# The order of wide and narrow matmuls in three of the seven quarter products of a feed-forward pair

## The chip, the cores and the metric

The kernel runs on one core of a Trainium2 chip. Its metric is the device time of one execution in microseconds; the profile comes from one further execution of the same program. TensorE is called PE below, VectorE DVE, ScalarE ACT, GpSimd POOL and SyncE SP, as the profile does.

## What is computed

One block of a streaming encoder on 512 frames of 1024 features, in float32: a feed-forward half step, a mixer (convolution module and gated linear attention), a second feed-forward half step, a gated embedding and a last norm. The change touches the feed-forward blocks alone, of which there are two:

```python
def _swiglu(x, w_in, w_out):
    gate, up = jnp.split(x @ w_in, 2, axis=-1)
    return (jax.nn.silu(gate) * up) @ w_out
...
h = h + 0.5 * _swiglu(_rmsnorm(h, ffn1_norm[i]), ffn1_w_in[i], ffn1_w_out[i])
...
h = h + 0.5 * _swiglu(_rmsnorm(h, ffn2_norm[i]), ffn2_w_in[i], ffn2_w_out[i])
```

`x` is 512 x 1024, `w_in` 1024 x 5632 (gate and up side by side) and `w_out` 2816 x 1024.

## The kernel before

**Two parts for each operand.** A float32 value is held as a high part (rounded by an ACT copy) and a low part (what is left, by a DVE subtraction). A product is high by high, high by low and low by high. For weights the tiles are `wh` and `wl`, each in a ring of six buffers.

**Pairs.** The hidden width 2816 is worked through in 11 pairs of 128-column blocks, each with its gate and its up columns. For a pair the 2 x 2 block product (gate and up rows by the two halves of the frames) is formed by a scheme with seven quarter products in place of eight: `m1`, `m2`, `m6`, `m7`, `m5`, `m4`, `m3`, in this order. Each multiplies a 512 x 256 piece of weights (raw, or a sum of pieces: `s1` to `s4`) with a 512 x 256 piece of activations (raw, `hg` in the rows of the profile, or a sum, `t1` to `t4`, shown as `t`). Results are kept in PSUM tiles of two banks (`pd`): `m1`, `m6`, `m5` and `m3` add into `p.x`, `m7` and `m4` into `p.w`, and `m2` stands in `p.y`.

**Late pairs.** From the third pair of the scheme on, a pair is "wide" (`p.wide`), and a quarter product is 16 matmuls written by `mul2`: eight *wide* ones, in which one high weight block `wh` (128 x 128) meets the high and low part of the activations side by side (512 columns), then eight *narrow* ones, in which the low block `wl` meets the high part alone (256 columns, into the first half of the same bank). Each matmul loads a weight block of its own. The first block has seven late pairs (4 to 10) and the second eight (3 to 10), 15 in all. Earlier pairs go through `mul`, where everything is 256 columns wide, unless the tile has two banks.

**What stands around.** After `m5` and after `m3` a late pair has an output piece: 24 matmuls with `w_out`, 512 columns each, into tiles `ps` (`second`). In rows of the profile these are `ps<-act,wh` and the like. After `m1`, `m6` and `m5` ACT copies `p.x` out of PSUM (`snap`), and after `m3` it copies a half of it; DVE adds these to `p.y` and `p.w` (`plus`).

**What sets the order.** `drive` runs the units (a quarter product or an output piece) in a list; it calls a unit's preparation, the high and low part of its weights, four units ahead (`AHEAD`; five for `m5`). Every PE, DVE and ACT instruction is chained behind the one recorded before it, so each engine keeps the order in which the code is written. Weights come by DMA issued from SP.

Of the kernel before, what the change touches and what calls it, by code (L numbers as in the profile page):

```python
# [31 lines left out]
HALF = SEQ // 2  # L32
# [30 lines left out]
def block_kernel(ctx: ExitStack, tc: tile.TileContext, a: dict, out: bass.AP):  # L63
    nc = tc.nc
    pe, dve, act, pool = (Ordered(tc, e) for e in (nc.tensor, nc.vector, nc.scalar, nc.gpsimd))
# [39 lines left out]
    def tmp(s, w=SEQ, dt=F32, bufs=2):  # L105
        return tp.tile([P, w], dt, tag=s, bufs=bufs, name=nm(s))
# [20 lines left out]
    def bank():  # L127
        if mode[0] == 0:
            turn_no[0] += 1
            at = turn_no[0] % 7  # L130
            if at in (3, 4):
                return fixed()
            if at in (5, 6):
                return spare()
        return psum(singles(), 3, [P, SEQ])
# [37 lines left out]
    first_of, at = {}, 0  # L173
# [49 lines left out]
    def high(r3):  # L223

        nk, nc_ = r3.shape[1], r3.shape[2]
        hi = wp.tile([P, 1024], F32R, tag="wh", bufs=6, name=nm("wh"))
        lo = wp.tile([P, 1024], F32R, tag="wl", bufs=6, name=nm("wl"))
        h3 = hi[:, :nk * nc_].rearrange("p (k c) -> p k c", k=nk)
        l3 = lo[:, :nk * nc_].rearrange("p (k c) -> p k c", k=nk)
        act.copy(h3, r3)  # L230
        return h3, l3, r3
# [116 lines left out]
    def mul(ps, w, x, first, last, ks=range(4)):  # L348

        (wh, wl), k0 = w, ks[0]  # L350
        for k in ks:
            xh, xl = x[k][:2]
            for i in range(2):
                cs = slice(i * P, (i + 1) * P)
                o = ps[:, i * HALF:(i + 1) * HALF]
                end = last and k == ks[-1] and i == 1
                pe.matmul(o, wh[:, k - k0, cs], xh, start=(first and k == ks[0] and i == 0), stop=False, skip_group_check=True)
                pe.matmul(o, wh[:, k - k0, cs], xl, start=False, stop=False, skip_group_check=True)
                pe.matmul(o, wl[:, k - k0, cs], xh, start=False, stop=end, skip_group_check=True)

    def two(t):
        return t.rearrange("p (k c) -> p k c", k=2)

    def mul2(ps, w, x, first, last):

        if len(ps.shape) == 2:
            return mul(ps, w, x, first, last)
        wh, wl = w
        at = [(k, i, slice(i * P, (i + 1) * P)) for k in range(4) for i in range(2)]
        for k, i, cs in at:  # L370
            pe.matmul(two(ps[:, i]), wh[:, k, cs], x[k][2], start=(first and k == 0), stop=False, skip_group_check=True)
        for k, i, cs in at:
            pe.matmul(ps[:, i, 0:HALF], wl[:, k, cs], x[k][0], start=False, stop=last and k == 3, skip_group_check=True)

    def sub(out, x, y):
        dve.tensor_tensor(out=out, in0=x, in1=y, op=ALU.subtract)
# [233 lines left out]
    def ffn(w_in, w_out, x, gname, given, first, rsb, hooks, plain, far={}, casts={}, adds=()):  # L610
# [6 lines left out]
        start = 1 + len(plain)  # L617
# [6 lines left out]
        def row(i):  # L624
            return got['rsb'][:, i * HALF:(i + 1) * HALF].unsqueeze(1).to_broadcast([P, 2, HALF])

        def times_row(src, i, name):
            o = tmp(name)
            dve.tensor_tensor(out=two(o), in0=two(src), in1=row(i), op=ALU.mult)
            return o  # L630

        def silu(g):
            s = tmp("s")
            act.activation(s, g, AF.Silu)
            return s

        def plus(ps, t, i, name):
            o = tmp(name)
            if len(ps.shape) == 2:
                dve.tensor_tensor(out=o, in0=ps, in1=t, op=ALU.add)  # L640
            elif len(t.shape) == 2:
                dve.tensor_tensor(out=two(o), in0=ps[:, :, 0:HALF], in1=two(t), op=ALU.add)
                dve.tensor_tensor(out=two(o), in0=ps[:, :, HALF:], in1=two(o), op=ALU.add)
            else:
                dve.tensor_tensor(out=t, in0=ps, in1=t, op=ALU.add)
                dve.tensor_tensor(out=two(o), in0=t[:, :, 0:HALF], in1=t[:, :, HALF:], op=ALU.add)
            dve.tensor_tensor(out=two(o), in0=two(o), in1=row(i), op=ALU.mult)
            return o
# [11 lines left out]
        def snap(ps, name, rest=None):  # L660
            if name == "sq":
                o = rest if rest is not None else two(tmp(name, 2 * SEQ))
                if len(ps.shape) == 2 and rest is None:
                    act.copy(o[:, 0], ps)
                else:
                    act.copy(o, ps)
                return o
            o = tmp(name, bufs=1)
            act.copy(o, ps)
            return o  # L670

        def gated(p, s, u, i):
            if not hasattr(p, "m"):
                p.m = tmp("m", 2 * SEQ, bufs=1).rearrange("p (f c) -> p f c", f=2)
            dve.tensor_tensor(out=p.m[:, :, i * HALF:(i + 1) * HALF], in0=two(u), in1=two(s), op=ALU.mult)

        def act_parts(p):
            c = [c for c, (f0, f1) in enumerate(CUTS) if f0 <= p.f < f1][0]
            to = cvt if c % 2 == 0 and p.f == CUTS[c][0] else bt
            p.acts = [split(p.m[:, f, :], "act", to) for f in range(2)]  # L680
# [31 lines left out]
            return [gate0]  # L712

        def m6(p):
            mul2(p.x, p.part("s2"), x.op["t2"], False, False)
            p.u2 = snap(p.x, "sq" if p.wide else "u2")

        def m7(p):
# [1 line left out]
            mul2(p.w, p.part("s3"), x.op["t3"], True, False)  # L720

        def m5(p):
            mul2(p.x, p.part("s1"), x.op["t1"], False, False)
            p.u = plus(p.w, snap(p.x, "sq", None if p.wide else p.both[:, 1]), 1, "u1")

        def m4(p):
# [1 line left out]
            gated(p, p.s0, plus(p.w, p.u2, 0, "u1"), 0)  # L728

        def m3(p):  # L730
            mul2(p.x, p.part("s4"), x.op["b22"], False, True)
            if p.wide:
                o = tmp("g1")
                act.copy(two(o), p.x[:, :, 0:HALF])
                dve.tensor_tensor(out=two(o), in0=p.x[:, :, HALF:], in1=two(o), op=ALU.add)
                dve.tensor_tensor(out=two(o), in0=two(o), in1=row(1), op=ALU.mult)
                if p is not pairs[end]:
                    after["m6", p.f // 2 + 1] = [lambda: act_parts(p)]

                def gate1():  # L740
                    p.s1 = silu(o)

                return [gate1, lambda: gated(p, p.s1, p.u, 1)] + ([lambda: act_parts(p)] if p is pairs[end] else [])
            elif p is pairs[start] and not plain:
                o = times_row(p.x, 1, "g1")
                after["m6", p.f // 2 + 1] = [lambda: gated(p, silu(o), p.u, 1), lambda: act_parts(p)]
                return []
            else:
                s = silu(times_row(p.x, 1, "g1"))
            if p is pairs[end]:  # L750
                return [lambda: gated(p, s, p.u, 1), lambda: act_parts(p)]
            after["m6", p.f // 2 + 1] = [lambda: act_parts(p)]
            return [lambda: gated(p, s, p.u, 1)]
# [305 lines left out]
    ps = bank()  # L1059
    for k0 in range(0, DC, 4):  # L1060
        for i in range(2):
            for j in range(4):
                pe.matmul(ps[2 * RANK * j:2 * RANK * (j + 1)], gw[:, k0 + j, :], hg[k0 + j][i].bitcast(F32),
                          start=(k0 == i == 0), stop=(k0 + i == 5), skip_group_check=True)
# [13 lines left out]
    for j in range(2):  # L1078
        ps = bank()
# [13 lines left out]
    cums, epos, eneg, edec, decay, ends = [], [], [], [], [], []  # L1093
# [77 lines left out]
    def tokblock(w, t, mid={}):  # L1171

        ps = bank()
        ts = slice(t * P, (t + 1) * P)
        i = 0
        for k in range(DC):
            wh, wl = w[k // 2][:2]
            xh, xl = hg[k]
            for x, y in ((xh, wh), (xl, wh), (xh, wl)):
                if i in mid:  # L1180
                    mid[i]()
                pe.matmul(ps, x[:, ts], y[:, k % 2, :], start=(i == 0), stop=(i == 3 * DC - 1))
                i += 1
        return ps
# [90 lines left out]
    for t in range(TB):  # L1275
        ps = tokblock(wv, t, {5: lambda: chunk_sums(range(6)),
                             8: lambda: wr.append(high(raw_r[2])),
                             14: lambda: wr.append(high(raw_r[3]))} if t == 3 else {})
# [57 lines left out]
    for t in range(TB):  # L1336
        if t == 0:
            taps(3)
            ps = tokblock(wr, t, {5: lambda: chunk_sums([6]), 12: lambda: outputs(0)})
            chain(range(4, 7))  # L1340
            oload(4)
        elif t == 1:
            ps = tokblock(wr, t, {2: lambda: outputs(1)})
# [8 lines left out]
        else:  # L1352
            ps = tokblock(wr, t)
# [116 lines left out]
    for k in range(4):  # L1470
        for n in range(3):
            w, ps = half[n]
            wh, wl = rows_of(w, k)
# [68 lines left out]
    q11, q21, q12, q22, b11, b21, t2, wproj = ([] for _ in range(8))  # L1542

    def narrow(tag, bufs, s_):
        return wp.tile([P, 1024], F32, tag=tag, bufs=bufs, name=nm(s_)).rearrange("p (k c) -> p k c", k=2)
# [6 lines left out]
    praw, s1, n2, gfin = [], [], [], []  # L1552
# [235 lines left out]
    t1, t3 = q11, q12  # L1788
# [46 lines left out]
    b22 = [added(later_high(t)) for t in q22]  # L1835
# [75 lines left out]
```

## Time and profile before

| | |
|---|---|
| device time, 3 runs | median 930.98 us (929.45 to 931.45) |
| the profiled execution | 929.6 us, span of its instructions 927.9 us |
| mean granted TensorE clock | 0.998 |
| first block's late pairs | from about 113 to 319 us of the span |
| second block's late pairs | from about 600 to 837 us of the span |
| wide matmuls of quarter products, `pd<-hg,wh` and `pd<-t,wh` | 576 and 392, mean 391 and 392 ns |
| narrow ones, `pd<-hg,wl` and `pd<-t,wl` | 512 and 392, mean 282 ns |
| DVE, ACT, POOL busy | 823.0, 507.8, 58.3 us |

Matmuls are pipelined: a row of the profile lasts from a matmul's start until its last result is written, and the next one has long started by then. So the mean of 391 ns is not what a matmul costs PE. Cost is read from the distance between the starts of two rows, divided by the number of matmuls between them. Rows of the timeline are merged: "x8" is eight matmuls in a row with the same operands.

### The profile page before, as it was taken

How to read it: one execution, taken by the hardware profiler on the slowest of the kernel's cores; microseconds unless marked ns; L12 is line 12 of the kernel's file. 1: busy time of each engine (PE TensorE's matmuls, PEld its weight loads, DVE VectorE, ACT ScalarE, POOL GpSimd, SP SyncE). 2: the span in 40 equal slices, each digit the busy share in tenths (PEclk: the TensorE clock that was granted, in tenths of full speed). 3: DMA queues.
4: the chain of work that ended last, by engine and by line, in shares of the span. 5: the costliest groups of instructions: out<-in, count | busy, mean ns of one | idle time of the engine just before them, and what ended most of it. 6: DMA issues, size and time to landing. Idle time of an engine off the chain costs nothing.

```text
span 927.9 us, 12878 instructions
## 1 busy us (share of the span) xinstructions
PE 918.3 (99%) x4982; PEld 782.4 (84%) x4982; DVE 823.0 (89%) x1098; ACT 507.8 (55%) x740; POOL 58.3 (6%) x73
## 2 busy tenths in 40 slices
PE   9999999999999999999999999999999999999996
PEld 8898888888888888788877889888888888888885
DVE  6699989999999876999986789899999999997896
ACT  7664355445444574463564875355445444456883
POOL 0120000000000111001120020000000000000120
PEclk9999999999999999999999999999999999999999
DMA  9433334224322693356552563334224322348463
GB/s 325 116 91 120 108 115 128 88 80 133 118 91 65 155 260 93 74 130 138 137 137 75 153 141 109 114 114 125 87 85 130 120 91 78 110 136 244 91 113 115
DMA packets 104175, 114.44 MB, mean 123 GB/s; under 512 B 3889, under 2 KB 90289, under 8 KB 104113
## 3 DMA queue, kind: packets, MB, share of 16 engines
q1 hardware_dynamic: 97664, 94.65, 32.8%
q0 software_dynamic: 6304, 18.88, 11.2%
q8 instruction: 39, 0.64, 0.3%
q14 instruction: 24, 0.19, 0.1%
q10 hardware_dynamic: 144, 0.09, 0.0%
HBM read 93.67 MB, written 2.10 MB: 103 GB/s over the span
## 4 chain that ended last, share of the span: by engine, by line
PE 99%; DVE 1%; issue 0%; ACT 0%; POOLq 0%; DVEq 0%
PE ps L46 59%; PE pd L46 40%; DVE u L46 0%; DVE rs L46 0%; ACT yc L46 0%; DVE y L46 0%; DVE g L46 0%; DVE s L46 0%; DVE yc L46 0%; POOLq L1907 0%; DVE ms L46 0%; DVE zeros L46 0%; DVE sse L46 0%; DVEq L46 0%; POOLq L46 0%
## 5 line engine op out<-in xcount | busy, mean ns | idle before, releaser
L46 DVE TENSOR_TENSOR wl<-wr,wh 128x1024 fp32r<-128x1024 f32 (+2 forms) x161 | 188.3, 1180 | 16.3 <-ACT wh L46 16.1
L46 ACT CAST wh<-wr 128x1024 fp32r<-128x1024 f32 (+2 forms) x178 | 176.2, 1021 | 20.7 <-PE ps L46 6.4
L46 PE MATMUL pd<-hg,wh 128*128 128x512 f32 x576 | 150.0, 391 | 0.0
L46 PE MATMUL ps<-act,wh 128*128 128x512 f32 x448 | 138.3, 390 | 0.0
L46 PEld LDWEIGHTS pd<-hg,wh 128*128 128x128 f32 x576 | 105.9, 188 | 21.0 <-DVE u L46 0.4
L46 PE MATMUL ps<-hg,wh 128*128 128x512 f32 (+1 forms) x448 | 117.3, 346 | 0.0
L46 PE MATMUL pd<-t,wh 128*128 128x512 f32 x392 | 98.2, 392 | 0.0
L46 PEld LDWEIGHTS ps<-act,wh 128*128 128x128 f32 x448 | 83.1, 188 | 16.5
L46 ACT ACTIVATE s<-g 128x512 f32<-128x512 f32 x48 | 30.4, 633 | 117.9 <-DVE g L46 117.9
L46 ACT COPY sq<-pd 128x1024 f32<-128x1024 f32 x45 | 45.7, 1016 | 87.3 <-PE pd L46 52.9
L46 PEld LDWEIGHTS ps<-hg,wh 128*128 128x128 f32 x448 | 78.0, 190 | 11.3 <-issue 1.3
L46 PE MATMUL ps<-act,wl 128*128 128x512 f32 x224 | 87.1, 389 | 0.0
L46 PE MATMUL pd<-hg,wl 128*128 128x256 f32 (+1 forms) x544 | 83.9, 289 | 0.0
L46 PEld LDWEIGHTS pd<-hg,wl 128*128 128x128 f32 x544 | 75.9, 190 | 6.3
L46 PEld LDWEIGHTS pd<-t,wh 128*128 128x128 f32 x392 | 70.5, 189 | 12.6
L46 PE MATMUL ps<-hg,wl 128*128 128x512 f32 (+1 forms) x224 | 77.1, 344 | 0.0
L46 ACT CAST wh<-sm 128x1024 fp32r<-128x1024 f32 x42 | 44.0, 1051 | 54.7 <-DVE sm L46 50.5
L46 PEld LDWEIGHTS pd<-t,wl 128*128 128x128 f32 x392 | 53.5, 190 | 3.8
L46 DVE TENSOR_TENSOR wl<-sm,wh 128x1024 fp32r<-128x1024 f32 x42 | 50.9, 1219 | 4.9 <-ACT wh L46 4.9
L46 DVE TENSOR_TENSOR sq<-pd,sq 128x1024 f32<-128x1024 f32 x45 | 54.8, 1218 | 0.4 <-PE pd L46 0.4
L46 PE MATMUL ps<-wh,hg 128*128 128x512 f32 x176 | 54.8, 392 | 0.0
L46 PE MATMUL pd<-t,wl 128*128 128x256 f32 x392 | 54.7, 282 | 0.0
(307 smaller groups left out, 1636.9 us busy)
## 6 DMA issues: line engine op xcount, KB each, us to landing
wr<-in_ffn_w_in SPq DMA_DIRECT2D x84, 512.0 KB, 3.7
wr<-in_ffn_w_out SPq DMA_DIRECT2D x32, 512.0 KB, 3.5
wr<-in_w_in SPq DMA_DIRECT2D x20, 512.0 KB, 5.1
wl<-wr POOLq DMA_DIRECT2D x18, 512.0 KB, 5.3
wr<-in_ffn_w_out SPq DMA_DIRECT2D x16, 384.0 KB, 3.1
wr<-in_w_out SPq DMA_DIRECT2D x8, 512.0 KB, 4.0
wq<-in_ple_w_gate SPq DMA_DIRECT2D x8, 512.0 KB, 3.8
wl<-wq POOLq DMA_DIRECT2D x8, 512.0 KB, 4.9
```

The source lines that it names most:

```text
L46: inst = call(*args, **kwargs)
```

## The change

`mul2` gets a switch `narrow_first`. With it the eight narrow matmuls of a quarter product are issued ahead of the eight wide ones, and the closing mark moves to the wide ones. `m6`, `m5` and `m3` set it; `m1`, `m2`, `m7` and `m4` do not. What is multiplied and where it is added stay the same.

```diff
-    def mul2(ps, w, x, first, last):
+    def mul2(ps, w, x, first, last, narrow_first=False):
 
         if len(ps.shape) == 2:
             return mul(ps, w, x, first, last)
         wh, wl = w
         at = [(k, i, slice(i * P, (i + 1) * P)) for k in range(4) for i in range(2)]
-        for k, i, cs in at:
-            pe.matmul(two(ps[:, i]), wh[:, k, cs], x[k][2], start=(first and k == 0), stop=False, skip_group_check=True)
-        for k, i, cs in at:
-            pe.matmul(ps[:, i, 0:HALF], wl[:, k, cs], x[k][0], start=False, stop=last and k == 3, skip_group_check=True)
+
+        def wide(ends):
+            for k, i, cs in at:
+                pe.matmul(two(ps[:, i]), wh[:, k, cs], x[k][2], start=(first and k == 0), stop=ends and k == 3, skip_group_check=True)
+
+        def narrow(ends):
+            for k, i, cs in at:
+                pe.matmul(ps[:, i, 0:HALF], wl[:, k, cs], x[k][0], start=False, stop=ends and k == 3, skip_group_check=True)
+
+        for run, ends in ((narrow, False), (wide, last)) if narrow_first else ((wide, False), (narrow, last)):
+            run(ends)
...
         def m6(p):
-            mul2(p.x, p.part("s2"), x.op["t2"], False, False)
+            mul2(p.x, p.part("s2"), x.op["t2"], False, False, True)
...
         def m5(p):
-            mul2(p.x, p.part("s1"), x.op["t1"], False, False)
+            mul2(p.x, p.part("s1"), x.op["t1"], False, False, True)
...
         def m3(p):
-            mul2(p.x, p.part("s4"), x.op["b22"], False, True)
+            mul2(p.x, p.part("s4"), x.op["b22"], False, True, True)
```

The order on PE at the head of `m6` in the second late pair of the first block: `pd_1469` is `m2`'s tile, `pd_1443` the pair's `p.x`, `pd_1528` its `p.w`; `wh` is a high weight part, `wl` a low one, and the last number is the moving operand's width. A row with x4 is four matmuls.

```order
 L46 MATMUL pd_1469<-hg_264,wl_1353 128x256 x2
 L46 MATMUL pd_1469<-hg_285,wl_1353 128x256 x2
+L46 MATMUL pd_1443<-t_92_481,wl_1381 128x256 x4
+L46 MATMUL pd_1443<-t_93_484,wl_1381 128x256 x4
 L46 MATMUL pd_1443<-t_92_481,wh_1380 128x512 x4
 L46 MATMUL pd_1443<-t_93_484,wh_1380 128x512 x4
-L46 MATMUL pd_1443<-t_92_481,wl_1381 128x256 x4
-L46 MATMUL pd_1443<-t_93_484,wl_1381 128x256 x4
 L46 MATMUL pd_1528<-t_98_509,wh_1408 128x512 x4
 L46 MATMUL pd_1528<-t_99_512,wh_1408 128x512 x4
```

The low blocks of `m6` moved up behind the low blocks of `m2`, and its high blocks now stand directly ahead of the high blocks of `m7`.

Further on in the same pair, `m7` (`pd_1528`) is followed by `m5` (`pd_1443`) and an output piece (`ps_1585`).

```order
 L46 MATMUL pd_1528<-t_98_509,wl_1409 128x256 x4
 L46 MATMUL pd_1528<-t_99_512,wl_1409 128x256 x4
+L46 MATMUL pd_1443<-t_108_555,wl_1405 128x256 x4
+L46 MATMUL pd_1443<-t_109_558,wl_1405 128x256 x4
 L46 MATMUL pd_1443<-t_108_555,wh_1404 128x512 x4
 L46 MATMUL pd_1443<-t_109_558,wh_1404 128x512 x4
-L46 MATMUL pd_1443<-t_108_555,wl_1405 128x256 x4
-L46 MATMUL pd_1443<-t_109_558,wl_1405 128x256 x4
 L46 MATMUL ps_1585<-act_970,wh_1465 128x512 x2
 L46 MATMUL ps_1585<-act_970,wl_1466 128x512
```

Here too low blocks now meet low blocks, and `m5` ends with 512-column matmuls, of which kind the whole output piece is.

At the end of a pair, `m4` (here `pd_1266`) is followed by `m3` (`pd_1179`); these are the rows of the changed kernel, in the first late pair of the first block.

```order
L46 MATMUL pd_1266<-hg_181,wl_1233 128x256 x2
L46 MATMUL pd_1266<-hg_202,wl_1233 128x256 x2
L46 MATMUL pd_1179<-hg_221,wl_1263 128x256 x2
L46 MATMUL pd_1179<-hg_242,wl_1263 128x256 x2
L46 MATMUL pd_1179<-hg_264,wl_1263 128x256 x2
L46 MATMUL pd_1179<-hg_285,wl_1263 128x256 x2
L46 MATMUL pd_1179<-hg_221,wh_1262 128x512 x2
L46 MATMUL pd_1179<-hg_242,wh_1262 128x512 x2
L46 MATMUL pd_1179<-hg_264,wh_1262 128x512 x2
L46 MATMUL pd_1179<-hg_285,wh_1262 128x512 x2
L46 MATMUL ps_1414<-act_970,wh_1287 128x512 x2
```

Before, the four rows with `wl_1263` stood behind the four with `wh_1262`, directly ahead of the output piece. The number of matmuls of each kind is the same, and so is the order on DVE, ACT, POOL and SP.

## The prediction

> **What bounds the kernel now.** I read the page first, then who waits for whom on PE, then the chain of work that ended last, and at the end the timeline of one late pair.
>
> ```profile
> PE 918.3 (99%) x4982; PEld 782.4 (84%) x4982; DVE 823.0 (89%) x1098; ACT 507.8 (55%) x740; POOL 58.3 (6%) x73
> ...
> PE 99%; DVE 1%; issue 0%; ACT 0%; POOLq 0%; DVEq 0%
> ```
>
> The last of these rows is the chain's share by engine: 99% of the span hangs on PE. DVE is busy for 89%, but that alone doesn't make it a bound. What PE waited for, over the whole span:
>
> ```profile
> PE ps L46 <- DVE zeros L46: 1.1, 1, 1.1
> PE ps L46 <- ACT yc L46: 0.2, 1, 0.2
> ```
>
> Two waits, 1.3 us in total, neither in a late pair. So in the late pairs nothing but PE's own pace counts. The chain shows that pace in the second block; each late pair opens with a piece of 80 matmuls (`m1`, `m2`, `m6`, `m7`, `m5`):
>
> ```profile
> 600.40 13.94 PE pd L46 x80
> 614.34 5.47 PE ps L46 x24
> 619.81 5.56 PE pd L46 x32
> 625.37 5.47 PE ps L46 x24
> 630.83 13.94 PE pd L46 x80
> ...
> 813.43 13.94 PE pd L46 x80
> ```
>
> From 600.40 to 813.43 are seven pairs, so one takes 213.03 / 7 = **30.433 us**, for 80 + 24 + 32 + 24 = 160 matmuls: 104 wide (seven products of eight, two output pieces of 24) and 56 narrow.
>
> **What one matmul costs, and what a switch costs.** The timeline of one late pair, first column the start: an output piece behind `m3` of the pair before, then `m1`, `m2` and `m6`, each first wide, then narrow.
>
> ```profile
> 198.78 0.40 PE L46 MATMUL ps<-actH,wh 128*128 128x512 f32 x1
> ...
> 200.17 0.61 PE L46 MATMUL ps<-act,wh 128*128 128x512 f32 x2
> ...
> 204.25 1.98 PE L46 MATMUL pd<-hg,wh 128*128 128x512 f32 x8
> 206.06 1.11 PE L46 MATMUL pd<-hg,wl 128*128 128x256 f32 x8
> 207.02 2.00 PE L46 MATMUL pd<-hg,wh 128*128 128x512 f32 x8
> 208.86 1.12 PE L46 MATMUL pd<-hg,wl 128*128 128x256 f32 x8
> 209.81 2.00 PE L46 MATMUL pd<-t,wh 128*128 128x512 f32 x8
> 211.65 1.11 PE L46 MATMUL pd<-t,wl 128*128 128x256 f32 x8
> ```
>
> Between 200.17 and 204.25 stand 18 wide matmuls: 4.08 / 18 = 0.2267 us each. The six ahead of them, from 198.78, take 1.39 us where six at that pace would take 1.36. The same 0.03 us shows in the products: `m1`, behind a wide output piece, needs 206.06 - 204.25 = 1.81 us for its eight wide ones (8 x 0.2267 = 1.81), while `m2` and `m6`, each behind narrow ones, need 1.84. So **wide behind narrow costs some 0.03 us once**, and the rest of the run goes at full pace. For the narrow ones I take a stretch of an early pair where all are narrow (21 matmuls between the first two rows):
>
> ```profile
> 551.16 0.28 PE L46 MATMUL ps<-hg,wl 128*128 128x256 f32 x1
> ...
> 553.68 0.28 PE L46 MATMUL ps<-hg,wl 128*128 128x256 f32 x1
> ...
> 560.64 2.00 PE L46 MATMUL pd<-t,wh 128*128 128x512 f32 x8
> 562.48 0.76 PE L46 MATMUL pd<-t,wl 128*128 128x256 f32 x5
> ```
>
> 2.52 / 21 = 0.120 us each. Eight behind wide ones take 0.96 or 0.95 us above (`m1`, `m2`) against 8 x 0.120 = 0.96: a switch the other way costs nothing, or gives a few ns back.
>
> The two together come out finer from the pair: 104 x 0.2267 + 56 x 0.120 = 23.57 + 6.72 = 30.29 us, and it takes 30.433. The 0.14 us left belong to the seven times that wide stands behind narrow in a pair (inside a product before the change narrow follows wide; at the head of `m2`, `m6`, `m7`, `m5`, of the piece behind it, of `m3` and of the piece behind that, wide follows narrow). 0.14 / 7 = **0.020 us** for one switch there and back. Since 0.2267 is known to some 0.0005 us (0.01 us of 18), this is 0.013 to 0.027; the direct reading, 1.84 against 1.81, gives 0.03, or 0.025 if 5 ns come back.
>
> **The change, part by part.** Nothing is removed or added: 24 wide and 24 narrow matmuls of a late pair change places. What goes is switches. Before, narrow is followed by wide seven times in a pair. With `m6`, `m5` and `m3` turned round, `m2`'s narrow ones run into `m6`'s, `m6`'s wide ones into `m7`'s, `m7`'s narrow ones into `m5`'s, `m5`'s wide ones into the output piece, `m4`'s narrow ones into `m3`'s, `m3`'s wide ones into the next piece. Wide behind narrow is left four times: at `m2`'s head and inside `m6`, `m5`, `m3`. Three fewer in each of 15 late pairs makes 45, which is also what the whole order on PE gives: 118 such places before, 73 after. The sum: 45 x 0.020 = **0.90 us less**, 0.42 in the first block (21) and 0.48 in the second (24).
>
> On the Trainium skill: "TensorE: Matmul & The Clock Gate", section "Back-to-back issue gap", has the distance of two warm matmuls as their columns over 2.4 GHz plus 2.5 ns, 216 ns at 512 and 109 ns at 256. By this rule a distance depends on the matmul alone and no order of the same matmuls could change the time, so the sum would be 0. The trace has 227 and 120 ns, and 1.84 against 1.81 us for eight equal ones, so it disagrees.
>
> **What is asked for earlier.** A narrow matmul needs the low part `wl`, which DVE makes, and in the three products PE now asks for it at the product's start, eight wide ones (1.84 us) sooner. DVE's rows for `m6`, `m5` and `m3` of the pair that opens at 204.25, in this order, and PE's for the starts of `m5` and `m3` (`m6` starts at 209.81 above):
>
> ```profile
> 203.17 1.22 DVE L46 TENSOR_TENSOR wl<-sm,wh 128x1024 fp32r<-128x1024 f32 x1
> ...
> 205.64 1.22 DVE L46 TENSOR_TENSOR wl<-sm,wh 128x1024 fp32r<-128x1024 f32 x1
> ...
> 215.84 1.23 DVE L46 TENSOR_TENSOR wl<-wr,wh 128x1024 fp32r<-128x1024 f32 x1 [0.18 <-ACT wh L46]
> ```
>
> ```profile
> 215.40 2.00 PE L46 MATMUL pd<-t,wh 128*128 128x512 f32 x8
> ...
> 226.42 1.78 PE L46 MATMUL pd<-hg,wh 128*128 128x512 f32 x7
> ```
>
> `m6`'s low part is done at 204.39, 5.4 us ahead of the product's start; `m5`'s at 206.86, 8.5 us; `m3`'s at 217.07, 9.4 us. The other late pairs repeat this one; none has less than 5.4 us. So I cost the earlier need at nothing: four units of preparation hide it. If this cover were gone, a product could lose up to the 1.84 us.
>
> The high part `wh` is read to the product's end now, 0.96 us later, and its buffer is free that much later for ACT's copy six weights on. The tightest of these follows `m3`, whose wide run from 226.42 ends some 2.0 us on (as long as the row at 215.40), at 228.4:
>
> ```profile
> 230.85 1.05 ACT L46 CAST wh<-wr 128x1024 fp32r<-128x1024 f32 x1
> ```
>
> That copy starts 2.4 us behind the release, so the later release is covered too, and costs at most 0.96 us of ACT's time where it weren't. A product still ends with the same 16 matmuls, so `snap`, `plus` and all behind them come at the same distance. DVE, ACT, POOL and SP keep their order; their work is set off by PE's ends and moves with them.
>
> **Against which time.** The profiled execution took 929.6 us (1.7 of it around the span). Less 0.90 that is 928.7. The runs shown have a median of 930.98, 1.4 above it, and reach from 929.45 to 931.45; the mean of all four is 930.4. From the median I get 930.1, from the mean 929.5, and forecast **929.8 us**. The runs differ by 0.2% among themselves, so a measurement tells no less than 0.2% (1.9 us) from no change, and the forecast of 0.1% lies within that.
>
> **Rivals.**
>
> 1. *The slow wide ones come from the head of a product, not from the switch.* In the kernel before, wide follows narrow only where a product or a piece begins, and PE waits for semaphores there. Then reordering inside a product removes nothing: 0 us, about 930.4. Against it: `m1` at 204.25 is a head as well and takes 1.81 us. This is also the outcome that the page's rule gives.
>
> 2. *Narrow runs of 16 leave a larger debt.* If a wide run pays for the number of narrow ones ahead, the four switches left cost up to twice as much for `m6`, `m5`, `m3`: 45 x 0.03 = 1.35 us more, which eats the gain and ends 0.45 above, near 930.8. Against it: at 560.64 a wide run starts behind 12 us of nothing but narrow ones and takes 562.48 - 560.64 = 1.84 us, as behind eight.
>
> 3. *Slower: the low part comes late.* The place is the first narrow matmul of `m6`, `m5` or `m3`; it decides from the point where DVE runs 5.4 us later than here. What PE loses at a head whose release comes just in time is seen once in the trace, in an early pair:
>
> ```profile
> 588.99 2.11 PE L46 MATMUL pd<-hg,wh 128*128 128x512 f32 x8
> 590.94 1.11 PE L46 MATMUL pd<-hg,wl 128*128 128x256 f32 x8
> ```
>
> 1.95 us for eight wide ones in place of 1.81: 0.14 us. At all 45 heads that is 6.3 us, less 0.9: 935.8 from the mean. At `m6` alone (15) it is 2.1 less 0.9, 931.6. Against it speaks the 5.4 us.
>
> 4. *More than the switches.* The direct reading of 0.03 gives 45 x 0.03 = 1.35 us, about 929.0, still within 0.2%. A gain over 1.9 us would need 0.042 us a switch, which no row shows; only the scatter of the runs could make it look so.
>
> **How the numbers follow.** The forecast with its 0.9 us (0.6 to 1.35) has a chance of 0.80, the first rival 0.08, the second 0.03, the third 0.04, the fourth beyond its 1.35 us 0.05. Time from each: the forecast's band runs from 930.4 - 1.35 = 929.0 to 930.98 - 0.6 = 930.4; the scatter of three runs about their median, 0.5 to 1.5 us, widens this to 928.5 to 931.2, which takes in the first two rivals. Faster by over 0.2% is the fourth and some scatter on the forecast: 0.08. Slower is the third and a little scatter: 0.04. Within 0.2%: 0.88.
>
> **What would show it.** In the changed profile a late pair should take 30.37 us (30.433 - 0.060). The wide ones of `m7`, and the output pieces behind `m5` and `m3`, should go at 0.2267 from the first one (1.81 for eight, 5.44 for a piece, not 5.47), the wide ones inside `m6` should still take 1.84, and 16 narrow ones 1.91 to 1.92. PE should have no wait in the late pairs. The prediction is wrong if a narrow run at the head of `m6`, `m5` or `m3` takes over 0.97 us for eight (rival 3), if the inner wide runs take over 1.86 (rival 2), or if the run of 8 in `m7` still takes 1.84 (rival 1).

## The result and the profile after

| | before | changed |
|---|---|---|
| device time, 18 runs each | 930.34 us (929.45 to 931.45) | 928.92 us (928.01 to 929.78) |
| the profiled execution | 929.6 us, span 927.9 | 928.9 us, span 927.2 |
| ratio | 1 | 0.9983 (95% interval 0.9977 to 0.9990) |

The changed kernel takes 1.42 us less at the median, and by the ratio 0.17%, inside the forecast range; 0.90 us and 0.1% were forecast. The interval reaches from 0.9 to 2.1 us, so the forecast gain lies at its lower end. The page and PE's waits read as before:

```profile
PE 917.6 (99%) x4982; PEld 782.9 (84%) x4982; DVE 822.8 (89%) x1098; ACT 507.7 (55%) x740; POOL 58.3 (6%) x73
...
PE 99%; DVE 1%; issue 0%; ACT 0%; POOLq 0%; DVEq 0%
```

```profile
PE ps L46 <- DVE zeros L46: 1.1, 1, 1.1
PE ps L46 <- ACT yc L46: 0.2, 1, 0.2
```

No wait of PE has come in, so the low parts are in time at the turned products. The chain of work that ended last shows the second block's late pairs:

```profile
600.07 13.93 PE pd L46 x80
613.99 5.44 PE ps L46 x24
619.43 5.57 PE pd L46 x32
625.00 5.44 PE ps L46 x24
630.44 13.93 PE pd L46 x80
...
812.68 13.93 PE pd L46 x80
```

Seven pairs from 600.07 to 812.68 take 212.61 us, **30.373 us** each, against 30.433 before: 0.060 less, three switches of 0.020. The output pieces, behind wide matmuls now, went from 5.47 to 5.44. The timeline of the pair that begins at 204.27 shows where the rest of the switches sits:

```profile
206.88 2.00 PE L46 MATMUL pd<-hg,wh 128*128 128x512 f32 x8
208.72 1.11 PE L46 MATMUL pd<-hg,wl 128*128 128x256 f32 x8
209.67 1.12 PE L46 MATMUL pd<-t,wl 128*128 128x256 f32 x8
210.63 3.82 PE L46 MATMUL pd<-t,wh 128*128 128x512 f32 x16
214.28 2.08 PE L46 MATMUL pd<-t,wl 128*128 128x256 f32 x16
216.20 2.00 PE L46 MATMUL pd<-t,wh 128*128 128x512 f32 x8
218.04 0.39 PE L46 MATMUL ps<-actH,wh 128*128 128x512 f32 x1
```

The second and third row are the 16 narrow matmuls of `m2` and `m6` (1.91 us), the fourth the 16 wide ones of `m6` and `m7`: 3.65 us, that is 16 x 0.2267 and 0.03 once, where two runs of eight had it twice. `m5`'s wide ones, behind 16 narrow ones, take 1.84.

### The profile page after: what moved, and what is told of

The parts are those of the page before. It is cut to its first block, busy times and chain, and to the rows that moved or that the text cites. A ratio compares the mean times of both kernels' runs of the same rounds, so it can differ in the third digit from the quotient of the medians.

```text
span 927.2 us, 12891 instructions
## 1 busy us (share of the span) xinstructions
PE 917.6 (99%) x4982; PEld 782.9 (84%) x4982; DVE 822.8 (89%) x1098; ACT 507.7 (55%) x740; POOL 58.3 (6%) x73
## 4 chain that ended last, share of the span: by engine, by line
PE 99%; DVE 1%; issue 0%; ACT 0%; POOLq 0%; DVEq 0%
PE ps L46 59%; PE pd L46 40%; DVE u L46 0%; DVE rs L46 0%; ACT yc L46 0%; DVE y L46 0%; DVE g L46 0%; DVE s L46 0%; DVE yc L46 0%; POOLq L1914 0%; DVE ms L46 0%; DVE zeros L46 0%; DVE sse L46 0%; DVEq L46 0%; POOLq L46 0%
## 5 line engine op out<-in xcount | busy, mean ns | idle before, releaser
L46 PE MATMUL pd<-t,wh 128*128 128x512 f32 x392 | 95.3, 391 | 0.0
L46 PE MATMUL pd<-hg,wl 128*128 128x256 f32 (+1 forms) x544 | 81.6, 289 | 0.0
L46 PEld LDWEIGHTS pd<-hg,wl 128*128 128x128 f32 x544 | 73.9, 191 | 5.1
L46 PE MATMUL pd<-t,wl 128*128 128x256 f32 x392 | 52.5, 283 | 0.0
L46 PEld LDWEIGHTS pd<-t,wl 128*128 128x128 f32 x392 | 50.6, 192 | 1.5
```

Of the source, the lines that this page charges most:

```text
L46: inst = call(*args, **kwargs)
```

## The experiments

In these kernels wide and narrow matmuls of quarter products stand in another order; everything else is the same.

**The change once more (e1) and the changed code without its marks (e2).** The first is the changed kernel itself; in the second, each engine's order is that of before:

```diff
-            mul2(p.x, p.part("s2"), x.op["t2"], False, False, True)
+            mul2(p.x, p.part("s2"), x.op["t2"], False, False)
...
-            mul2(p.x, p.part("s1"), x.op["t1"], False, False, True)
+            mul2(p.x, p.part("s1"), x.op["t1"], False, False)
...
-            mul2(p.x, p.part("s4"), x.op["b22"], False, True, True)
+            mul2(p.x, p.part("s4"), x.op["b22"], False, True)
```

> The changed kernel once more, beside fresh runs of the kernel before. Theory (45 switches from narrow to wide at 0.020 us each are gone, and nothing else): 0.90 us less than before, ratio 0.9990, and a late pair every 30.373 us. Rival (there is a further gain that the late pairs don't show): 1.4 us less again, ratio 0.9985, with the difference in some other stretch.

> The changed code with narrow_first set nowhere, so that every engine has the order of the kernel before. Both theories: the time of before, ratio 1.0000, a late pair every 30.433 us. What it deviates from 1 is what chance alone does to such a ratio (I expect up to 0.0005, 0.5 us); if it shows about 0.9995, the part of the measured gain beyond 0.90 us is no effect of the order.

Measured: e1 ratio 0.9984 (0.9975 to 0.9993), e2 1.0003 (0.9994 to 1.0012). The gain is the order's. It came out above 0.90 us a second time (930.65 to 929.13), as the rival has it, though 0.9990 lies in e1's interval. The means of the executions differ by 1.45 us in the first measurement (18 against 18) and by 1.58 here (33 against 11), so the part beyond 0.90 is more than scatter. Where it may come from is told with the further profiles below.

**All seven products turned (e3).** `mul2` opens a tile with the first narrow matmul, and `p.wide` is passed as `narrow_first` in `m1` to `m7`:

```diff
-                pe.matmul(two(ps[:, i]), wh[:, k, cs], x[k][2], start=(first and k == 0), stop=ends and k == 3, skip_group_check=True)
+                pe.matmul(two(ps[:, i]), wh[:, k, cs], x[k][2], start=(first and k == 0 and not narrow_first), stop=ends and k == 3, skip_group_check=True)
...
-                pe.matmul(ps[:, i, 0:HALF], wl[:, k, cs], x[k][0], start=False, stop=ends and k == 3, skip_group_check=True)
+                pe.matmul(ps[:, i, 0:HALF], wl[:, k, cs], x[k][0], start=(first and k == 0 and narrow_first), stop=ends and k == 3, skip_group_check=True)
```

> All seven quarter products of the late pairs have their narrow matmuls in front (m1, m2 and m7 open their tile with a narrow one then). Wide follows narrow 118 times in the program, as before the change: seven times in a late pair, only inside the products and no longer at their heads. Theory (the switch costs, wherever it stands): no change against before, a late pair every 30.433 us, 930.3 us. Rival (narrow first is what saves, 0.020 us a product, whatever its neighbours are): 7 x 0.020 less for a late pair, 30.293 us, 15 x 0.14 = 2.1 us less, ratio 0.9977. Rival (the cost belongs to a product's head): the same 30.293 us.

Measured: ratio 0.9998 (0.9989 to 1.0006). The chain's first and last piece of 80 in the second block:

```profile
602.26 13.97 PE pd L46 x80
...
815.29 13.97 PE pd L46 x80
```

213.03 / 7 = 30.433 us, as before the change. Narrow first alone brings nothing; the slow wide ones have moved from the heads of the products into them (eight wide ones inside a product take 1.84 us, and the output pieces behind wide ones 5.44), and both rivals fall.

**Another set turned (e6).** With the same `mul2`, `m2`, `m7`, `m5` and `m3` get `p.wide`, and `m6` is left wide first.

> In the late pairs m2, m7, m5 and m3 have their narrow matmuls in front, in place of m6, m5 and m3: other products, but wide follows narrow four times in a pair as well (inside the four). Theory (only the number of switches between long runs counts): a late pair every 30.373 us as with the change, 0.90 us less than before, ratio 0.9990. Rival (it matters which products are turned): any other period.

Measured: ratio 0.9987 (0.9978 to 0.9996).

```profile
599.77 13.93 PE pd L46 x80
...
812.38 13.93 PE pd L46 x80
```

212.61 / 7 = 30.373 us, as with the change. Between these two sets it does not matter which products are turned; four switches are left, and four are paid.

**Shorter runs (e4, e5, e9).** Here each quarter product that has both kinds mixes them: two wide and two narrow in turn, one and one, or four and four.

```diff
-        for k, i, cs in at:
-            pe.matmul(two(ps[:, i]), wh[:, k, cs], x[k][2], start=(first and k == 0), stop=False, skip_group_check=True)
-        for k, i, cs in at:
-            pe.matmul(ps[:, i, 0:HALF], wl[:, k, cs], x[k][0], start=False, stop=last and k == 3, skip_group_check=True)
+        for k in range(4):
+            for i in range(2):
+                cs = slice(i * P, (i + 1) * P)
+                pe.matmul(two(ps[:, i]), wh[:, k, cs], x[k][2], start=(first and k == 0), stop=False, skip_group_check=True)
+            for i in range(2):
+                cs = slice(i * P, (i + 1) * P)
+                pe.matmul(ps[:, i, 0:HALF], wl[:, k, cs], x[k][0], start=False, stop=last and k == 3, skip_group_check=True)
```

That is e4; in e5 the two matmuls stand in one loop over `k` and `i`, and in e9 the halves `k` = 0, 1 and `k` = 2, 3 follow each other.

> Every quarter product that has wide and narrow matmuls goes two wide, two narrow, four times over: wide follows narrow 457 times in the program in place of 118, 28 times in a late pair in place of 7. Theory: each of the 21 more switches of a pair costs, at the least, what the first two wide ones behind narrow ones lose (0.016 us) less the 0.0075 that the first narrow ones give back, 0.008 us, and at the most the full 0.020: a late pair takes 30.61 to 30.85 us, and the program is 2.9 to 6.8 us slower (339 switches), ratio 1.003 to 1.007. Rival (order costs nothing): 30.433 us, ratio 1.000.

> Every quarter product that has both kinds goes one wide, one narrow, eight times over: wide follows narrow 56 times in a late pair in place of 7. Two by two, a switch came to only (30.387 - 30.293) / 28 = 0.0034 us. Theory (what costs is a lead that PE spends in a run of narrow ones and earns back in the first five wide ones; runs too short to spend it cost little): one by one the lead is hardly touched, a late pair takes 30.29 to 30.36 us (0 to 0.001 us a switch), 15 x 0.07 to 0.14 = 1.1 to 2.1 us less than before, ratio 0.9977 to 0.9988. Rival (each switch costs its 0.0034 whatever the run): 30.293 + 56 x 0.0034 = 30.48 us, 0.7 us slower than before.

> Every quarter product that has both kinds goes four wide, four narrow, twice: wide follows narrow 14 times in a late pair. Measured so far above 30.293 us: 7 switches of runs of eight 0.140, 28 of runs of two 0.094, 56 of runs of one 0.400. Theory (a long narrow run spends a lead, and five wide ones earn it back): the first four wide ones lose 0.023 us and the first two narrow ones give back 0.007, but shorter runs stay below that, as two by two did (0.0034 in place of 0.008): 0.005 to 0.016 us a switch, a late pair of 30.36 to 30.52 us. Rival (a cost per switch that doesn't depend on the run, 0.020 us): 30.573 us.

The chain's first and last piece of 80 in the second block, of e4, of e5 and of e9:

```profile
601.85 13.92 PE pd L46 x80
...
814.56 13.92 PE pd L46 x80
```

```profile
602.71 14.12 PE pd L46 x80
...
817.56 14.12 PE pd L46 x80
```

```profile
601.92 14.01 PE pd L46 x80
...
815.89 14.01 PE pd L46 x80
```

| order | wide behind narrow in a pair | a pair, us | above 30.293 | for each, on average |
|---|---|---|---|---|
| before, e3: runs of 8 | 7 | 30.433 | 0.140 | 0.020 |
| the change, e6: runs of 8 and 16 | 4 | 30.373 | 0.080 | 0.020 |
| e9: runs of 4 | 14 | 30.567 | 0.274 | 0.020 |
| e4: runs of 2 | 28 | 30.387 | 0.094 | 0.0034 |
| e5: runs of 1 | 56 | 30.693 | 0.400 | 0.0071 |

(The last two columns are worked out from the third; 30.293 is 104 x 0.22667 + 56 x 0.120.) e4's time is that of before (ratio 0.9995, 0.9986 to 1.0004), where I had expected 1.003 to 1.007; e5 is slower, 1.0045 (1.0031 to 1.0058), where I had expected 0.9977 to 0.9988. e9 was executed once, 932.21 us against 930.85 for one execution of before beside it. In runs of eight and more a switch costs 0.020 us, in runs of two it nearly vanishes, and in runs of one it comes back by a third. The picture of a lead that is spent and earned back, which I formed after e4, gave the wrong sign for e5, and for e9 it named 30.52 us at most where 30.567 was measured. The flat cost named 30.573 for e9, but the mean of 0.020 there hides two sizes. The first two rows are of e9's timeline in the first block, the third is a row of its chain in the second:

```profile
207.25 1.09 PE L46 MATMUL pd<-hg,wh 128*128 128x512 f32 x4
...
218.47 0.40 PE L46 MATMUL ps<-actH,wh 128*128 128x512 f32 x1
```

```profile
615.93 5.49 PE ps L46 x24
```

Between the first two rows stand eight rounds of four wide and four narrow matmuls: 11.22 / 8 = 1.4025 us each, 0.016 above 4 x 0.22667 + 4 x 0.120. The output piece, 24 wide ones behind four narrow ones, takes 5.49 us where it takes 5.44 behind wide ones. So the twelve switches of a pair that lead into four wide ones cost 0.016 each, the picture's upper end, and the two that lead into an output piece some 0.04 (0.05 less what the narrow ones give back). That the mean is 0.020 again is a coincidence: a cost that depends on neither run is shown for runs of 8 and more, not for runs of four. In e5 the pieces take 5.46 to 5.47 and in e4 5.45, so the last column is an average there as well. No order takes less than the 30.373 us of the change.

**Further profiles for the stretch between the two blocks (e7, e8, e10, e11, e12).** Three are of the order of before (the kernel of e2) and two of the change (the kernel of e1), each with no other edit and one execution.

> The order of before once more, for one profile. In its last profile PE lost 1.16 us at 347 to 355 us of the span, where a weight transfer landed late and ACT, DVE and PE waited in turn; in the first profile of before it lost nothing there. If the part of the measured gain beyond 0.90 us comes from this stall being commoner without the change, this run should show it (PE's rows 1800 to 1900 take 23.0 us with it, 21.8 without); if it comes and goes alike in both, either outcome.

> The change once more, for one profile. If the stall is rare with the change, PE's rows 1800 to 1900 take 21.8 us, as in both of its profiles so far; if it comes and goes alike in both orders, either outcome.

> The order of before, a further profile for the stall between PE's rows 1800 and 1900 (21.81 us without it). So far it was 0 and 1.17 and 0.74 us with this order, and 0, 0 and 0.18 us with the change. If the change makes it rarer, this run has it (over 22.4 us); if it is chance alone, either outcome.

> As the run before it: the order of before, the same question; over 22.4 us for PE's rows 1800 to 1900 if the change makes the stall rarer, either outcome if it is chance alone.

> The change, a further profile: under 22.1 us for PE's rows 1800 to 1900 if the change makes the stall rarer, either outcome if it is chance alone.

("PE's rows 1800 to 1900" are the starts of its matmuls of these numbers, counted in order of time.) In e2, PE comes to the projection `ps<-hg,wa` and waits for DVE, which it did not in the first profile of before. The timeline of PE there, first in e2, then in before:

```profile
347.43 4.77 PE L46 MATMUL ps<-hg,wa 128*128 128x512 f32 x19
352.49 0.73 PE L46 MATMUL ps<-hg,wa 128*128 128x512 f32 x2 [0.29 <-DVE hg L46]
```

```profile
347.74 5.60 PE L46 MATMUL ps<-hg,wa 128*128 128x512 f32 x24
```

The rows behind DVE's delay are one of ACT and one of DVE in e2; the last fence has the same copy of ACT in before:

```profile
340.62 1.05 ACT L46 CAST wh<-wr 128x1024 fp32r<-128x1024 f32 x1 [2.63 <-DMA wr<-in_w_in]
...
342.33 1.42 DVE L46 SCALAR_TENSOR_TENSOR hg<-h,col,hg 128x512 fp32r<-128x512 f32 x2 [1.27 <-ACT hg L46]
```

```profile
339.54 1.05 ACT L46 CAST wh<-wr 128x1024 fp32r<-128x1024 f32 x1 [1.30 <-PE pd L46]
```

ACT stands 2.63 us in front of a weight tile that has not landed, its next work (`hg`) comes late, DVE waits 1.27 us for that, and PE in the end for DVE. In e10, which has no stall, ACT waits 0.46 us for the same tile; in e3, e4, e5 and e9 it waits 2.3 to 2.8 us. The stalls of e7 and e11 began elsewhere: ACT does not wait in front of that copy, but 1.72 and 1.90 us for an earlier weight tile, ahead of copies to `wa`, where it waits 1.06 us in before. So ACT waits longer than usual for a weight tile ahead of each of these stalls, but not for the same tile. DMA is full in this stretch; e2 by windows:

```profile
330.00:340.00 10.00, 10.00 (x46) 8.29 (x45) 6.59 (x10) 7.61 (x12) 3.49 (x4) 1.00 1.15 245
340.00:345.00 5.00, 5.00 (x24) 4.14 (x23) 3.73 (x5) 4.27 (x6) 0.00 (x0) 1.00 1.11 292
```

(The last two columns are the DMA engines' mean busy share, over 1 here, and GB/s. In the first profile of before, without the stall, the shares are 1.15 and 1.06, so a full DMA alone does not make the stall.) From the chain's rows of all nine profiles of the two orders, from the first block's first late pair to the second block's:

| order of before | us | the change | us |
|---|---|---|---|
| before | 113.11 to 600.40, 487.29 | after | 113.15 to 600.07, 486.92 |
| e2 | 112.70 to 601.14, 488.44 | e1 | 113.07 to 599.91, 486.84 |
| e7 | 113.92 to 601.91, 487.99 | e8 | 112.67 to 599.65, 486.98 |
| e10 | 113.06 to 600.32, 487.26 | e12 | 112.65 to 599.57, 486.92 |
| e11 | 112.84 to 600.76, 487.92 | | |
| mean | 487.78 | mean | 486.92 |

If the change made the stall rarer, e7, e10 and e11 were to show it and e8 and e12 not; e10 did not, the other four came out so. The means differ by 0.86 us. The 21 switches of this stretch make 0.42 of it; 0.45 are the stall, which three of five profiles without the change have (0.6 to 1.2 us) and none of four with it (0.2 at most). With the 24 switches of the second block, 0.48, that adds up to 1.35 us, close to the 1.42 of the medians (the whole spans of these profiles differ by 1.52 on average; the other 0.2 lies ahead of the first late pair).

The stall was also there in e3, e4, e5 and e9 (0.8 to 1.3 us), but not in e6, which takes 486.85 us from 112.92 to 599.77. So none of the five profiles of orders with four switches in a pair has it, and seven of the nine others have it. Dealt out at random, seven stalls would spare those five in about one case in a hundred. But this grouping was made afterwards, e4 has the stall although its pairs are only 0.014 us longer than the change's, and no run here shows how the order in the late pairs would reach these transfers; a run that takes the transfers away wasn't tried. Whether the change makes the stall rarer stays open.

## Why the prediction was right

**The bound.** PE alone sets the pace of the late pairs, before and after: no wait in either, and each pair is shorter by just what PE saves.

**The sum, 45 x 0.020 = 0.90 us.** It held in the late pairs to the last digit that the chain has, which is better than the reading behind it: that had 0.013 to 0.027 for a switch, so the third digit is luck. A pair was to take 30.37 us and takes 30.373; the pieces 5.44, `m5`'s inner wide run 1.84, 16 narrow ones 1.91. The direct reading of 0.03 for a switch was the worse of the two: the narrow ones behind wide ones give a part back (by the starts of single matmuls the first five wide ones lose 27.5 ns and the first two narrow ones give back 7.5).

**The time.** The forecast of 929.8 us came out 0.9 us too high: 0.4 because the kernel before takes 930.34 at the median of 18 executions and not the 930.7 that the forecast started from, between the 930.98 of three and the mean of four, and 0.5 because more was gained than the sum. That a measurement tells no less than 0.2% from no change was too careful: with 18 executions of each, the interval of 0.10 to 0.23% lies clear of zero.

**What was asked for earlier.** The cover of 5.4 us for the low parts and 2.4 us for the high parts' buffers was enough; no turned product starts late.

**A distance that depends on the matmul alone.** By the formula in the section "Back-to-back issue gap" of "TensorE: Matmul & The Clock Gate" in the Trainium skill a distance depends on the matmul alone, and the sum would have been 0. The Trainium skill gives this formula there for an isolated matmul and says that in a stream of weight loads and matmuls both set the spacing. e5, e9 and before have the same matmuls in a pair, and 30.693, 30.567 and 30.433 us: here the order counts.

**The rivals.** Rival 1 (the head of a product) falls with e3, where heads follow wide ones and the pair still costs 30.433. Rival 2 (longer narrow runs, larger debt) falls with the changed profile: 16 narrow ones, and still 1.84. Rival 3 (late low parts) had no place in any profile. Rival 4 named the size that was measured at the median (1.35 us), but by a cost of 0.03 us a switch, and that falls: the pair shows 0.020. In the profiles the rest lies outside the late pairs.

**What the sum left out.** It took the rest of the program to move along rigidly. That holds for the profile that I worked from, which has no stall between the blocks; three of the four later profiles of the same order have one of 0.6 to 1.2 us, so that the mean execution before is slower than the one I worked from. The 0.5 us between 0.90 and 1.42 stand beside 0.45 us of stall in the profiles. That they are the same is argued from the sizes, not shown.

## What to carry to other kernels

Where one engine runs without a wait, the time can be taken apart to a few nanoseconds by counting its instructions and the changes of kind between them, over many equal periods of the chain. Here it paid to put equal kinds next to each other across the borders of products, and with runs of 8 and 16 what that gives was a matter of count, not of place. A single profile of a kernel with a stretch full of transfers may lack a stall that other executions of the same program have (three of five here); several profiles show it.

## What the hardware showed that I had not expected

Wide matmuls (512 columns) follow each other at 0.2267 us and narrow ones (256) at 0.120 us, and a change of kind costs 0.020 us there and back in runs of 8 and 16. With shorter narrow runs it depends on what follows: behind four narrow ones 0.016 ahead of four wide ones and some 0.04 ahead of 24; in runs of 2 it averages 0.0034 and in runs of 1 0.0071. In e5's trace the distances repeat with a period of three pairs of matmuls (0.358, 0.356 and 0.346 us for a narrow and a wide one, where 0.2267 + 0.120 is 0.347); what makes them do so stays open.

The start of the program differs from execution to execution: the 100th matmul begins between 22.3 and 23.9 us of the span in the profiles here, and all behind it moves with it.
